# A residual block in fp32: the second FFN with four plain tiles instead of five, x's block sums by accumulating DMAs, transposes in runs of eight

## The chip, the cores and the metric

The kernel runs on one core of one Trainium2 chip. The metric is the device time of one execution in microseconds; the time given for a kernel is the median of its runs.

## The reference

One layer of a streaming encoder, S = 512 tokens, D = 1024, FF = 2816, all in fp32:

```
x = x + 1/2 * swiglu_ffn(rmsnorm(x, ffn1_norm), ffn1_w_gate, ffn1_w_up, ffn1_w_down)
x = x + hybrid_mixer(rmsnorm(x, mix_norm), ...)      # attention in chunks and pooling, one output projection
x = x + 1/2 * swiglu_ffn(rmsnorm(x, ffn2_norm), ffn2_w_gate, ffn2_w_up, ffn2_w_down)
x = rmsnorm(x, final_norm)

rmsnorm(x, g)    = x * rsqrt(mean(x * x) + 1e-6) * g
swiglu_ffn(x)    = (silu(x @ w_gate) * (x @ w_up)) @ w_down
```

## The kernel before

Every product is taken in three matmuls (`mm3`, L208 to L210): each operand is split into a rounded part `hi` (ScalarE casts it, L154 or L157) and a rest `lo` (VectorE subtracts, L155 or L158), and hi x hi, lo x hi and hi x lo are accumulated.

Each FFN's up half works through 22 column tiles f of 128 gate and 128 up columns. The tiles come in two kinds. A **plain** tile takes eight k-steps of gate and eight of up, each on 512 tokens: 48 matmuls of 512 columns. A **half-size** tile treats gate and up as the columns of a 2 x 2 block product and uses seven block products instead of eight (A11, S1, S2, S3, A12, A22, S4, in Winograd's form): 84 matmuls of 256 columns. For that it needs sums of x's blocks, S1 = a21 - a22, S2 = S1 + a11, S3 = a11 + a21 and S4 = S2 - a12 up to signs, and of the weights' blocks. `PLAIN = (5, 5)` says how many tiles of either FFN are plain; the others are half-size.

The change is in the second FFN's **opening**: all its plain tiles, the norm's sums, and whatever the first half-size tile needs. Its order on TensorE, VectorE and ScalarE is the string `OPENING`, written out by hand, a token a step. `W i` splits weights i, `B i` is a block of the first two tiles (two k-steps of both, 24 matmuls), `P` one half (gate or up) of a later plain tile, `L` a quarter of the last one; `n` is a step of the norm, whose last writes `rb`, the factor of each token; `g`, `u`, `m` are a tile's gate, its up, and the sums of its output; `h` prepares the first half-size tile's weights, `F` fetches some, `O` opens output tiles. `p` takes one step off the list that `Norm.blocks` returns: eight scalings of x by rb and the gain into the tiles `aside` (L403), the sums of blocks, and the splits of S3 and S2 (tiles `xa`), S4 (`sa`) and of A11, A22, S1, A12 (`ha`, two instructions each for hi and lo).

After the opening the half-size tiles follow in a loop with its own written order. In each, `u` is copied from the bank of the first product (ScalarE, L721) before the third product adds to that bank.

While the opening runs, TensorE also transposes the x that came from the mixer: 32 transposes `by_token` (L1666), taken one by one off the list `further` by `block` and `last_block`, four into a bank, which ScalarE copies (L1671) and SP stores to `x_d`. GpSimd's queue carries the sums of the down weights in DRAM: `make_sums` issues a mark and two DMAs (L868) a tile, some of them accumulating, as `RATES` says.

Of the kernel before, what the change touches and what calls it, by code (L numbers as in the profile page):

```python
# [12 lines left out]
AF = mybir.ActivationFunctionType  # L13
ALU = mybir.AluOpType
# [6 lines left out]
KD = D // P  # L21
# [17 lines left out]

ROOM, AHEAD_OF_PARTS, ALIGN = 1024 + 128, 16, 64  # L40
OFF, OFF_AT = (0, 2, 6), 32
PLAIN = (5, 5)
RATES = [[2] * (n - 1) + [0] + [2] * (FF // P - n - 2) + [0] * 2 for n in PLAIN]
PROBS = 3
M_TILES = 16
# [14 lines left out]
ACT_FIX, DVE_FIX, QK_NORM, NORM = 0.09, 0.1, 3.7538, 3.08  # L60
AHEAD_AT = 8
OPENING = (
    "W1 n0 B0 n1 W2 n2 B1 W3 p B2 p p p p p p W4 p B3 g0 p g1 p u0 W5 u1 p m0 m1 O1 W6 W7 p p P20 P21 W8 "
    "P30 g2 p u2 m2 p P31 W9 g3 u3 m3 F0 F1 L0 h0 F2 h1 F3 L1 p h2 L2 p h3 p L3 h4 g4 h5 F4 p O0 "
)
AHEAD, NORM_AT, FILL_AT, QK_ROOT = 2, 3, 7, ()
RANKS = {
# [8 lines left out]
def layer(  # L76
# [225 lines left out]
    class Norm:  # L302
# [80 lines left out]
            nc.vector.scalar_tensor_tensor(self.rb, v, 1.5, y, op0=ALU.add, op1=ALU.mult)  # L383
            yield

        def blocks(self, pool, aside):

            x_lo, x_hi = (z[:, : 4 * S].rearrange("p (k c) -> p k c", c=S) for z in aside[:2])
            a11, a21 = x_lo[:, :, :HT], x_lo[:, :, HT:]
            a12, a22 = x_hi[:, :, :HT], x_hi[:, :, HT:]
            s2, s4, s1 = (
                z[:, at : at + 4 * HT].rearrange("p (k c) -> p k c", c=HT)
                for z, at in ((aside[0], 4 * S), (aside[1], 4 * S), (aside[2], 0))
            )
            self.a = [None] * 7  # L400

            def scale(k):
                nc.vector.scalar_tensor_tensor(  # L403
                    (x_lo, x_hi)[k // 4][:, k % 4], x[k], gain_sb[:, self.which, k : k + 1],
                    self.rb, op0=ALU.mult, op1=ALU.mult,
                )

            def add(dst, one, two, op):
                nc.vector.tensor_tensor(dst, one, two, op=op)

            def whole(i, src, make, sign=None):
                pair = [make().rearrange("p (k c) -> p k c", c=HT) for _ in range(2)]
                split(src, *pair, sign)
                self.a[i] = [[z[:, k] for k in range(4)] for z in pair]

            def halves(i, src):

                self.a[i] = [[], []]
                for k in (0, 2):
                    pair = [  # L420
                        hpool.tile([P, 2, HT], F32R, tag="h", name=name("ha")) for _ in range(2)
                    ]
                    split(src[:, k : k + 2], *pair)
                    for z, to in zip(pair, self.a[i]):
                        to.extend(z[:, j] for j in range(2))

            def by_x(i):
                return lambda: xpool.tile([P, 2 * S], F32R, tag=f"x{i.pop()}", name=name("xa"))

            def extra():  # L430
                return pool.tile([P, 4 * HT], F32R, tag="extra", name=name("sa"), bufs=2)

            free = [3, 2, 1, 0]
            return [(scale, k) for k in range(KD)] + [
                (add, s1, a21, a22, ALU.subtract),
                (add, s2, s1, a11, ALU.add),
                (add, a21, a11, a21, ALU.add),
                (whole, S3, a21, by_x(free), -1.0),
                (whole, S2, s2, by_x(free), -1.0),
                (add, s4, s2, a12, ALU.subtract),  # L440
                (whole, S4, s4, extra),
                (halves, A11, a11),
                (halves, A22, a22),
                (halves, S1, s1),
                (halves, A12, a12),
            ]


    def ffn_up(norm, wA, down, loaded, parts=(), aside=(), further=()):
# [24 lines left out]
        def block(w, kp):  # L474
            for kk in range(2):
                k = 2 * kp + kk
                for j in range(4):
                    mm3(first[j], cut(w, (kk * 4 + j) * P, P), norm.h[k], k == 0, k == KD - 1)
                    if kp:
                        for _ in range(min(1 + (j == 3), len(further))):  # L480
                            further.pop(0)()

        def nothing():
            pass
# [1 line left out]
        def blocks_of(aside=()):  # L486
            aside = list(aside) + [
                down.pool.tile(
                    [P, 6 * groups[g][1] * HT], F32, tag=f"acts{groups[g][0]}", name=name("aside")
                )  # L490
                for g in range(G - 3 + len(aside), G)
            ]
            todo.extend(norm.blocks(down.pool, aside))

        def read_in():
            for kp in range(KD // 2):
# [79 lines left out]
        def opening():  # L576

            banks, halves_of = {f: first[2 * f : 2 * f + 2] for f in range(2)}, {}
            raw = dict(enumerate(parts[1:], 1))
            w = {0: parts[0]}  # L580
            steps = norm.steps()

            def fetch_raw(i):
                if i < 2 * plain and i not in raw:
                    raw[i] = raw_of(wA[i])

            def prepare(i):
                w[i] = parts_of(raw[i])
                fetch_raw(i + 3)

            def last_block():
                for j in range(4):
                    for kk in range(2):
                        k = KD - 2 + kk
                        mm3(first[j], cut(w[3], (kk * 4 + j) * P, P), norm.h[k], False, k == KD - 1)
                        for _ in range(min(1 + kk, len(further))):
                            further.pop(0)()

            def tile_product(n, j):
                acc = bank()  # L600
                banks.setdefault(n, []).append(acc)
                for k in range(KD):
                    mm3(acc, cut(w[2 * n + j], k * P, P), norm.h[k], k == 0, k == KD - 1)

            def last_tile(part):
                n = plain - 1
                if part == 0:
                    banks[n] = [bank(), bank()]
                for k in range(2 * part, 2 * part + 2):
                    for j in range(2):  # L610
                        mm3(
                            banks[n][j], cut(w[2 * n + j], k * P, P), norm.h[k], k == 0, k == KD - 1
                        )

            def gate(f):
                g, sg = temp(), temp()
                nc.vector.tensor_tensor(g, banks[f][0], norm.rb, op=ALU.mult)
                nc.scalar.activation(sg, g, AF.Silu)
                halves_of[f] = sg

            def up(f):
                sg = halves_of[f]
                nc.vector.tensor_tensor(sg, sg, norm.rb, op=ALU.mult)
                down.place(f, banks[f][1], sg)

            def sums(f):
                down.sums(f)
                down.make_sums(halves_of[f], 2)

            def half_size(what):  # L630
                n = plain
                if what == 0:
                    high11(n)
                    low11(n)
                elif what == 1:
                    sum13(n)
                elif what == 2:
                    high13(n)
                    low13(n)
                elif what == 3:  # L640
                    sum24(n)
                elif what == 4:
                    high24(n)
                else:
                    low24(n)

            def loads(what):
                fetch(plain + what // 2, ("ra", "rb")[what % 2])

            do = {  # L650
                "W": prepare, "B": lambda i: block(w[i], i) if i < 3 else last_block(),
                "P": lambda i: tile_product(i // 10, i % 10), "L": last_tile, "g": gate, "u": up,
                "m": sums, "h": half_size, "F": loads, "n": lambda i: next(steps), "p": piece,
                "O": lambda i: down.open(range(1, G - 3) if i else range(G - 3, G)),
            }
            for token in OPENING.split():
                do[token[0]](int(token[1:] or 1))
            assert not todo and not further
            return partial(up, plain - 1), partial(sums, plain - 1)
# [149 lines left out]
    class Down:  # L809
# [37 lines left out]
        def begin(self, pool):  # L847
            self.pool, self.acts = pool, []
            self.raws, self.parts, self.pairs = {}, {}, {}
            self.n_products, self.loads, self.loads_from = 0, [], 4  # L850
            self.open(range(1))
            rooms[:] = [
                z for tag in ("ra", "rb") for z in ((wpool, "raw", RAW, 1024), (pool, tag, RAW, 2 * S))
            ]
            part_rooms[:] = [(wpool, HILO)] * HILO + [(pool, 1)]
# [1045 lines left out]
```

## Time and profile before

| | |
|---|---|
| time, median of 3 runs | 837.81 us (837.65 to 838.47) |
| the profiled execution's own time | 838.23 us |
| its span, first to last instruction | 836.5 us |
| TensorE busy, share of the span | 99% |
| VectorE, ScalarE, GpSimd | 85%, 60%, 18% |
| opening of the second FFN | 501.94 to 560.51 us of the span |
| its 17 half-size tiles | 560.51 to 722.77 us |
| its down half and the end | 722.77 to 836.4 us |

Durations of single instructions are in the timeline's rows; an engine starts the next of its instructions a little before the last one's recorded end, so a row of several gives the distance between two. A DMA's time runs from its issue to its landing.

### The profile page before, as it was taken

What the parts mean: (1) busy time and instruction counts of PE and PEld (TensorE: products, weight loads), DVE (VectorE), ACT (ScalarE), POOL (GpSimd) and SP (SyncE); (2) the same over time, 40 slices, a digit from 0 to 9 for tenths busy, and PEclk for the clock granted to TensorE, in tenths of its full rate; (3) what the DMA queues carried; (4) which work ended last, traced back from release to release, by engine and by line L of the source; (5) the groups of instructions that cost most, each with busy time, mean ns of one, the idle gap of its engine ahead of it and who ended that gap; (6) DMA issues with size and microseconds to landing.
All of it is one profiled execution on the core that took longest, in us unless ns stands there. A gap on an engine that the chain in (4) does not pass through costs nothing.

```text
span 836.5 us, 14350 instructions
## 1 busy us (share of the span) xinstructions
PE 826.8 (99%) x5288; PEld 740.3 (89%) x5288; DVE 712.0 (85%) x1157; ACT 501.8 (60%) x859; POOL 150.0 (18%) x212
## 2 busy tenths in 40 slices
PE   9999999999999999999999999999999999999996
PEld 7889999999988888887888887889999999988885
DVE  7999998899897678766979668989889999887896
ACT  8446555665675656558747745455566555756573
POOL 0312211222074000102111000111221121132600
PEclk9999999999999999999999999999999999999999
DMA  8667788888689973332221137757877888689922
GB/s 300 183 198 170 200 210 243 201 207 207 193 245 271 329 233 110 108 110 89 76 69 62 67 110 263 235 154 216 215 212 217 214 204 211 228 269 340 323 87 101
DMA packets 78839, 160.63 MB, mean 192 GB/s; under 512 B 7328, under 2 KB 30384, under 8 KB 78384
## 3 DMA queue, kind: packets, MB, share of 16 engines
q1 hardware_dynamic: 55680, 113.03, 40.1%
q0 software_dynamic: 22656, 46.14, 26.0%
q8 instruction: 41, 0.67, 0.3%
q10 hardware_dynamic: 432, 0.54, 0.2%
q14 instruction: 30, 0.25, 0.1%
HBM read 153.38 MB, written 50.34 MB: 244 GB/s over the span
## 4 chain that ended last, share of the span: by engine, by line
PE 97%; DMA 1%; DVE 1%; ACT 0%; SPq 0%; issue 0%; DVEq 0%
PE mm L208 23%; PE mm L210 23%; PE mm L209 23%; PE a L208 8%; PE a L209 8%; PE a L210 8%; PE a L1438 1%; PE a L1374 1%; PE a L1426 1%; DMA x<-in_xT_dram 1%; PE a L1296 0%; PE a L1666 0%; PE a L327 0%; PE a L1029 0%; PE mm L1029 0%; SPq L201 0%
## 5 line engine op out<-in xcount | busy, mean ns | idle before, releaser
L155 DVE TENSOR_TENSOR wlo<-raw,whi 128x1024 fp32r<-128x1024 f32 (+2 forms) x115 | 124.4, 1088 | 25.9 <-ACT whi L154 25.3
L154 ACT CAST whi<-raw 128x1024 fp32r<-128x1024 f32 (+2 forms) x115 | 107.3, 944 | 49.2 <-PE mm L210 13.0
L209 PE MATMUL mm<-ha,whi 128*128 128x256 f32 x408 | 112.8, 276 | 0.0
L208 PE MATMUL mm<-ha,whi 128*128 128x256 f32 x408 | 112.8, 276 | 0.0
L210 PE MATMUL mm<-ha,wlo 128*128 128x256 f32 x408 | 112.7, 276 | 0.0
L721 ACT ACTIVATE t<-mm 128x256 f32<-128x256 f32 x102 | 39.2, 384 | 114.3 <-PE mm L210 111.6
L531 DVE TENSOR_TENSOR wlo<-wsum,whi 128x1024 fp32r<-128x1024 f32 x68 | 83.0, 1220 | 11.0 <-PE mm L210 7.9
L866 POOL COPY mark<-t 128x1 f32<-128x1 f32 x44 | 14.3, 324 | 391.6 <-DVE t L774 243.0
L208 PE MATMUL mm<-hhi,whi 128*128 128x512 f32 x192 | 76.6, 401 | 0.9 <-ACT whi L154 0.6
L209 PEld LDWEIGHTS mm<-ha,whi 128*128 128x128 f32 x408 | 76.6, 188 | 0.1
L208 PEld LDWEIGHTS mm<-ha,whi 128*128 128x128 f32 x408 | 76.6, 188 | 0.1
L210 PEld LDWEIGHTS mm<-ha,wlo 128*128 128x128 f32 x408 | 76.6, 188 | 0.0
L209 PE MATMUL mm<-hlo,whi 128*128 128x512 f32 x192 | 74.9, 391 | 0.0
L210 PE MATMUL mm<-hhi,wlo 128*128 128x512 f32 x192 | 74.8, 391 | 0.0
L868 POOL DMA_DIRECT2D wsum<-in_wB_dram x72 | 71.1, 1102 | 12.3 <-issue 7.5
L526 ACT CAST whi<-wsum 128x1024 fp32r<-128x1024 f32 x68 | 67.9, 1047 | 2.0 <-PE mm L209 1.5
L209 PE MATMUL mm<-wlo,ah 128*128 128x512 f32 x176 | 68.5, 389 | 0.0
L210 PE MATMUL mm<-whi,ah 128*128 128x512 f32 x176 | 68.5, 389 | 0.0
L208 PE MATMUL mm<-whi,ah 128*128 128x512 f32 x176 | 68.4, 389 | 0.0
L531 DVE TENSOR_TENSOR wlo<-raw,whi 128x512 fp32r<-128x512 f32 x68 | 62.0, 950 | 0.0
L526 ACT CAST whi<-raw 128x512 fp32r<-128x512 f32 x68 | 56.2, 827 | 2.5 <-issue 2.5
L208 PE MATMUL a<-whi,ah 128*128 128x512 f32 (+1 forms) x154 | 55.7, 362 | 0.0
(233 smaller groups left out, 2398.7 us busy)
## 6 DMA issues: line engine op xcount, KB each, us to landing
raw<-in_wA_dram SPq DMA_DIRECT2D x136, 256.0 KB, 4.1
wsum<-in_wB_dram POOLq DMA_DIRECT2D x60, 512.0 KB, 6.9
raw<-wsum SPq DMA_DIRECT2D x40, 512.0 KB, 4.8
raw<-in_wB_dram SPq DMA_DIRECT2D x30, 512.0 KB, 7.4
wsum<-wsum POOLq DMA_DIRECT2D x20, 512.0 KB, 5.2
raw<-in_wA_dram SPq DMA_DIRECT2D x19, 512.0 KB, 4.1
x<-in_xT_dram SPq DMA_DIRECT2D x16, 256.0 KB, 8.8
raw<-in_wQK_dram SPq DMA_DIRECT2D x8, 512.0 KB, 3.5
```

The costliest lines, as they stand in the source:

```text
L154: nc.scalar.copy(hi, src)
L155: nc.vector.tensor_tensor(lo, src, hi.bitcast(F32), op=ALU.subtract)
L208: nc.tensor.matmul(acc, a[0], b[0], start=start, stop=False, **more)
L209: nc.tensor.matmul(acc, a[0], b[1], start=False, stop=False, **more)
L210: nc.tensor.matmul(acc, a[1], b[0], start=False, stop=stop, **more)
L526: nc.scalar.copy(hi, src)
L531: nc.vector.tensor_tensor(lo, src, hi.bitcast(F32), op=ALU.subtract)
L721: nc.scalar.activation(dst, src, AF.Copy, scale=scale)
L866: nc.gpsimd.tensor_copy(mark, after[:, 0:1])
L868: nc.gpsimd.dma_start(self.rows(i, g), self.rows(self.terms[i][at], g), **(dict(accum_op=ALU.add) if at else {}),)
L1374: nc.tensor.matmul(banks[i][:, at : at + n], qT[pair][0][a][rows, t * P : (t + 1) * P], kT[pair][0][b][rows, :n], start=a + b == 0, stop=a ...
L1426: nc.tensor.transpose(tp[:, n : n + P], prob[h, t][:, j * P : (j + 1) * P], ident)
```

## The change

The second FFN has four plain tiles and eighteen half-size ones; the first FFN is as it was. `blocks` gets a second list for the second FFN: each sum of blocks is begun by a scaled copy on ScalarE (`begin`) and completed by one accumulating DMA from SBUF to SBUF on GpSimd's queue (`onto`); S3 is added into a21 in place. `OPENING` is written anew for one tile fewer, and `block` takes eight transposes after each k-step of blocks 1 and 2, none in the last.

```diff
-PLAIN = (5, 5)
+PLAIN = (5, 4)
@@
-    "W1 n0 B0 n1 W2 n2 B1 W3 p B2 p p p p p p W4 p B3 g0 p g1 p u0 W5 u1 p m0 m1 O1 W6 W7 p p P20 P21 W8 "
...
+    "W1 n0 W2 B0 n1 W3 n2 p2 B1 B2 p8 W4 p2 B3 g0 p g1 u0 m0 u1 p W5 O1 W6 W7 p2 P20 P21 p g2 m1 F0 "
...
@@ blocks
+            def begin(dst, src, sign):
+                nc.scalar.activation(dst, src, AF.Copy, scale=sign)
+
+            def onto(dst, src):
+                nc.gpsimd.dma_start(dst, src, accum_op=ALU.add)
+
             free = [3, 2, 1, 0]
+            if by_dma:
+                return [(scale, k) for k in range(KD)] + [
+                    (begin, s1, a22, -1.0),
+                    (onto, s1, a21),
+                    (begin, s2, a11, 1.0),
+                    (onto, a21, a11),
+                    (onto, s2, s1),
+                    (begin, s4, a12, -1.0),
+                    (whole, S3, a21, by_x(free), -1.0),
+                    (whole, S2, s2, by_x(free), -1.0),
+                    (onto, s4, s2),
+                    (whole, S4, s4, extra),
+                    (halves, A11, a11),
+                    (halves, A22, a22),
+                    (halves, S1, s1),
+                    (halves, A12, a12),
+                ]
@@ block
-                    if kp:
-                        for _ in range(min(1 + (j == 3), len(further))):
-                            further.pop(0)()
+                for _ in range(min(2 * NT if kp else 0, len(further))):
+                    further.pop(0)()
@@ blocks_of
-            todo.extend(norm.blocks(down.pool, aside))
+            todo.extend(norm.blocks(down.pool, aside, loaded))
@@ last_block
-                        for _ in range(min(1 + kk, len(further))):
-                            further.pop(0)()
```

What moves, at three places. First TensorE, in block 1 of the opening, before (`xr` is the x to be transposed, `mm` the banks of the first two tiles, `a` the bank of transposes):

```order
L354 MATMUL a_6082<-t_6081,ones_r 128x512
L208 MATMUL mm_6066<-hhi_5953,whi_6074 128x512
L209 MATMUL mm_6066<-hlo_5954,whi_6074 128x512
L210 MATMUL mm_6066<-hhi_5953,wlo_6075 128x512
L1666 MATMUL a_6131<-ident_r,xr_6049 128x128
L208 MATMUL mm_6067<-hhi_5953,whi_6074 128x512
L209 MATMUL mm_6067<-hlo_5954,whi_6074 128x512
L210 MATMUL mm_6067<-hhi_5953,wlo_6075 128x512
L1666 MATMUL a_6131<-ident_r,xr_6049 128x128
```

And now, at the end of block 1's first k-step:

```order
L208 MATMUL mm_6069<-hhi_5953,whi_6074 128x512
L209 MATMUL mm_6069<-hlo_5954,whi_6074 128x512
L210 MATMUL mm_6069<-hhi_5953,wlo_6075 128x512
L1686 MATMUL a_6148<-ident_r,xr_6049 128x128 x4
L1686 MATMUL a_6156<-ident_r,xr_6049 128x128 x4
L208 MATMUL mm_6066<-hhi_5963,whi_6074 128x512
L209 MATMUL mm_6066<-hlo_5964,whi_6074 128x512
```

The transposes, one or two after every third matmul before, now stand eight together after twelve matmuls, and fill two banks at once.

Second GpSimd's queue in the opening, before (`mark` waits for a tile's gate or up; `wsum` are the down weights' sums in DRAM):

```order
L866 COPY mark_6307<-t_6285 128x1
L868 DMA wsum_138<-in_wB_dram 256x1x512
L868 DMA wsum_139<-in_wB_dram 256x1x512
L866 COPY mark_6316<-t_6290 128x1
L868 DMA wsum_138<-in_wB_dram 256x1x512
L868 DMA wsum_140<-in_wB_dram 256x1x512
```

And now (`aside_6051` holds a11, a21 and s2, `aside_6070` a12, a22 and s4, `aside_6071` s1):

```order
L437 DMA aside_6071<-aside_6051 128x4x256
L437 DMA aside_6051<-aside_6051 128x4x256
L437 DMA aside_6051<-aside_6071 128x1024
L886 COPY mark_6301<-t_6289 128x1
L888 DMA wsum_138<-in_wB_dram 256x1x512
L888 DMA wsum_139<-in_wB_dram 256x1x512
L437 DMA aside_6070<-aside_6051 128x1024
L886 COPY mark_6390<-t_6294 128x1
L888 DMA wsum_138<-in_wB_dram 256x1x512
```

Three adds stand ahead of the first mark, the fourth (S4's) behind the first two copies of the down weights' sums; what followed the marks before now follows the adds.

Third ScalarE at the end of the opening, before (`whi` from `wsum` or `raw` are the first half-size tile's weights, `t` from `t` a gate's silu, `t` from `mm` u's copy):

```order
L154 CAST sa_6434<-aside_6070 128x1024
L154 CAST whi_6463<-raw_6327 128x1024
L618 ACTIVATE t_6468<-t_6467 128x512
L526 CAST whi_6502<-raw_6482 128x512
L154 CAST ha_6527<-aside_6051 128x512
L154 CAST ha_6531<-aside_6051 128x512
L526 CAST whi_6535<-wsum_6509 128x1024
```

And now:

```order
L154 CAST sa_6431<-aside_6070 128x1024
L154 CAST ha_6441<-aside_6051 128x512
L154 CAST ha_6445<-aside_6051 128x512
L548 CAST whi_6473<-wsum_6428 128x1024
L154 CAST ha_6480<-aside_6070 128x512
L154 CAST ha_6484<-aside_6070 128x512
L154 CAST ha_6488<-aside_6071 128x512
L154 CAST ha_6492<-aside_6071 128x512
L548 CAST whi_6496<-wsum_6477 128x1024
L638 ACTIVATE t_6512<-t_6511 128x512
L154 CAST ha_6516<-aside_6070 128x512
L154 CAST ha_6520<-aside_6070 128x512
```

The split of S4, which stood ahead of the last plain tile's weights, now stands ahead of the splits of the other four operands and of the weight sums, and it reads what the fourth add writes; u's copy, in the row after the last shown, stands behind them all.

More of the change, by code (lines that the diff above doesn't have):

```diff
@@ L62 @@
 OPENING = (
-    "W1 n0 B0 n1 W2 n2 B1 W3 p B2 p p p p p p W4 p B3 g0 p g1 p u0 W5 u1 p m0 m1 O1 W6 W7 p p P20 P21 W8 "
-    "P30 g2 p u2 m2 p P31 W9 g3 u3 m3 F0 F1 L0 h0 F2 h1 F3 L1 p h2 L2 p h3 p L3 h4 g4 h5 F4 p O0 "
+    "W1 n0 W2 B0 n1 W3 n2 p2 B1 B2 p8 W4 p2 B3 g0 p g1 u0 m0 u1 p W5 O1 W6 W7 p2 P20 P21 p g2 m1 F0 "
+    "u2 m2 L0 F1 h0 h1 p F2 F3 p L1 L2 h2 h3 p2 h4 L3 g3 h5 p F4 O0 "
 )
@@ L384, in steps, with blocks @@
             yield
-        def blocks(self, pool, aside):
+        def blocks(self, pool, aside, by_dma=False):
             x_lo, x_hi = (z[:, : 4 * S].rearrange("p (k c) -> p k c", c=S) for z in aside[:2])
```

## The prediction

> **What bounds the kernel now.** The page comes first: how busy each engine is, and the chain of work that ended last.
>
> ```profile
> PE 826.8 (99%) x5288; PEld 740.3 (89%) x5288; DVE 712.0 (85%) x1157; ACT 501.8 (60%) x859; POOL 150.0 (18%) x212
> PE 97%; DMA 1%; DVE 1%; ACT 0%; SPq 0%; issue 0%; DVEq 0%
> ```
>
> TensorE is never idle for long and the chain is TensorE's: time goes only where it gets fewer or shorter matmuls, and comes only where another engine makes it wait. So I cut the span where the change lies, in the table of busy time by stretch (columns: length, then busy time and count of PE, PEld, DVE, ACT, POOL, then clock, DMA share and GB/s).
>
> ```profile
> 501.94:560.51 58.57, 58.57 (x275) 47.62 (x274) 51.42 (x65) 29.62 (x41) 6.77 (x12) 1.00 0.74 232
> 560.51:722.77 162.26, 162.26 (x1429) 162.26 (x1428) 148.07 (x225) 96.02 (x174) 29.13 (x48) 1.00 0.77 205
> 541.02:551.90 10.88, 10.88 (x50) 9.01 (x48) 8.39 (x12) 4.41 (x6) 2.65 (x5) 1.00 0.73 203
> ```
>
> The first row is the opening of the second FFN (five plain tiles, the norm's sums, 32 transposes), the second its 17 half-size tiles. PE is busy for all of both. The third row is one plain tile's length: 48 matmuls of 512 columns between two starts (the two further ones counted reach in from the ends), 10.88 us, 0.2267 each. A half-size tile takes 162.26 / 17 = 9.545 us for 84 matmuls, 0.1136 each. In the opening VectorE is busy for 51.42 of 58.57 us: it is the engine that would run out if the opening were simply made shorter.
>
> **The change part by part.** *One plain tile goes, one half-size tile comes*: -10.88 + 9.545 = **-1.3 us** of TensorE.
>
> *Transposes in runs of eight.* Where they stand now, in the timeline of PE (start, time, line, count); the last two rows are runs of four elsewhere in the program, on plain fp32:
>
> ```profile
> 507.38 0.62 PE L354 MATMUL a<-t,ones_r 128*128 128x512 f32 x2
> 507.84 0.39 PE L208 MATMUL mm<-hhi,whi 128*128 128x512 f32 x1
> ...
> 508.59 0.44 PE L208 MATMUL mm<-hhi,whi 128*128 128x512 f32 x1
> ...
> 509.40 0.45 PE L208 MATMUL mm<-hhi,whi 128*128 128x512 f32 x1
> ...
> 510.21 0.45 PE L208 MATMUL mm<-hhi,whi 128*128 128x512 f32 x1
> ...
> 510.96 0.28 PE L1666 MATMUL a<-ident_r,xr 128*128 128x128 f32 x2
> 511.08 0.46 PE L208 MATMUL mm<-hhi,whi 128*128 128x512 f32 x1
> ...
> 368.18 0.60 PE L1296 MATMUL a<-ident,t 128*128 128x128 f32 x4
> ...
> 369.32 0.60 PE L1296 MATMUL a<-ident,t 128*128 128x128 f32 x4
> ```
>
> From 508.59 to 509.40 lie three matmuls (0.68) and one transpose: 0.81, so a lone transpose costs 0.13. From 510.21 to 511.08 lie three matmuls and two transposes: 0.87, so the second costs 0.06. The norm's two sums take 507.84 - 507.38 = 0.46. All 32 transposes now cost 58.57 - 240 x 0.2267 - 0.46 = 3.7. A run of eight would cost 0.13 + 7 x 0.06 = 0.55, four runs 2.2. The other bound: the fp32 runs of four take 369.32 - 368.18 - 0.68 = 0.46, 0.115 each, and 32 of those are the 3.7 of now. I take the row of the same kind of transpose: **-1.5 us**, and keep 0 for the range.
>
> Without any wait the opening then ends 192 x 0.2267 + 0.46 + 2.2 = 46.2 us after 501.94, at 548.1, and the sum is -1.3 - 1.5 = **-2.8 us**.
>
> *The four adds leave VectorE.* They take 1.21 us each there; with two fewer weight splits (1.22 each) and one gate and up fewer VectorE loses some 9 of its 51.4 us while the opening shrinks by 12.4. That is what makes four plain tiles possible. ScalarE gains three copies (1.05 each) and loses two casts. The price is that three of the four adds now follow each other through the DMA queue: s1, then s2 = s1 + a11 (queued behind the add into a21), then s4 = s2 + a12. No run shows an accumulating DMA from SBUF to SBUF; the nearest rows of the DMA list are (out<-in, KB each, us from issue to landing):
>
> ```profile
> wsum<-in_wB_dram POOLq DMA_DIRECT2D x1, 512.0 KB, 4.3
> wsum<-in_wB_dram POOLq DMA_DIRECT2D x1, 512.0 KB, 6.4
> wsum<-in_wB_dram POOLq DMA_DIRECT2D x1, 512.0 KB, 7.8
> xr<-x SPq DMA_DIRECT2D x8, 256.0 KB, 2.6
> raw<-in_wA_dram SPq DMA_DIRECT2D x2, 256.0 KB, 3.5
> wsum<-in_wB_dram POOLq DMA_DIRECT2D x1, 512.0 KB, 6.6
> wsum<-in_wB_dram POOLq DMA_DIRECT2D x2, 512.0 KB, 7.5
> ```
>
> ```profile
> 616.56 2.13 POOL L868 DMA_DIRECT2D wsum<-in_wB_dram  x2 [0.25 <-issue]
> ```
>
> The rows are answers for short stretches of time. The first (529.8 to 530.3 us) is a plain copy on GpSimd's queue, the second (569.4 to 570.0) an accumulating one with little beside it, the third (534.3 to 534.9) an accumulating one beside SP's weight fetches. The fourth and fifth say what SBUF instead of DRAM saves: 2.6 against 3.5. The last two are a pair of accumulating ones, the first alone (6.6) and both (median 7.5, so the second took 8.4); GpSimd's timeline has them issued within 2.13 us, about 0.9 apart, so the second lands some 2.7 behind the first. So an add costs between 4.3 (adding is free) and 7.8; I take 6.4 less some 0.8 for SBUF, and 0.2 more for the fetches beside it: **5.8 us**, nearest to the 6.4.
>
> Now the walk. The first two blocks after the norm's sums end at 501.94 + 72 x 0.2267 + 0.46 + 2.2 = 520.9, and ScalarE copies the last transposes before it starts s1. These are the rows of ScalarE and VectorE on which this and the rest lie (where xN stands, N instructions run into each other; in brackets idle time ahead of a row and what ended it):
>
> ```profile
> 528.00 0.59 ACT L1671 COPY t<-a 128x512 f32<-128x512 f32 x1 [1.16 <-PE a L1666]
> 529.53 2.94 ACT L154 CAST whi<-raw 128x1024 fp32r<-128x1024 f32 x3
> 542.59 1.06 ACT L154 CAST sa<-aside 128x1024 fp32r<-128x1024 f32 x1 [0.45 <-DVE aside L409]
> 546.86 0.63 ACT L618 ACTIVATE t<-t 128x512 f32<-128x512 f32 x1 [2.26 <-DVE t L617]
> 561.33 1.13 ACT L154 CAST ha<-aside 128x512 fp32r<-128x512 f32 x2
> 562.36 0.37 ACT L721 ACTIVATE t<-mm 128x256 f32<-128x256 f32 x1
> 515.21 0.69 DVE L383 SCALAR_TENSOR_TENSOR rb<-t,t 128x512 f32<-128x512 f32 x1
> 516.95 4.73 DVE L403 SCALAR_TENSOR_TENSOR aside<-x,gain_sb,rb 128x512 f32<-128x512 f32 x7
> 535.07 2.35 DVE L155 TENSOR_TENSOR wlo<-raw,whi 128x1024 fp32r<-128x1024 f32 x2
> 541.35 1.21 DVE L409 TENSOR_TENSOR aside<-aside,aside 128x1024 f32<-128x1024 f32 x1
> 553.16 1.28 DVE L155 TENSOR_TENSOR ha<-aside,ha 128x512 fp32r<-128x512 f32 x2
> 560.03 0.69 DVE L617 TENSOR_TENSOR t<-mm,rb 128x512 f32<-128x512 f32 x1 [0.65 <-PE mm L210]
> ```
>
> The copy ends near 521.7, s1's start (1.05) at 522.8; VectorE's eight scalings (4.73 for seven, so 0.66 apart) follow rb, there at 515.9, and end at 521.2, in time. The first add lands at 522.8 + 5.8 = 528.6, the second at 534.4, the third 2.7 behind it at 537.1. The fourth is queued on GpSimd behind a mark and two 512 KB copies of the down weights' sums; these drain while it starts, and it lands at 537.1 + 5.8 = **542.9**.
>
> Behind it waits ScalarE, in a written order: S4's split (1.06), then eight casts of halves, two casts of weight sums, the last gate's silu and the copy of u. On VectorE stand S4's rest (2.35 - 1.22 = 1.13), two halves (0.6 each), a weight sum's rest 1.13, two sums (1.2), four halves (2.4), the last gate (0.69); then ScalarE's silu 0.54 until the next can start, two casts (1.03) and u's copy (0.37). In sum 1.06 + 1.13 + 1.2 + 1.13 + 1.2 + 2.4 + 0.69 + 0.54 + 1.03 + 0.37 = 10.8, with hops of about 0.1 between engines 11.1. TensorE's third product writes on into the bank that u's copy reads, so it cannot start before 542.9 + 11.1 = 554.0. By itself it would start two products after the opening: 548.1 + 24 x 0.1136 = 550.9. So TensorE waits **3.1 us** there. VectorE, 91% busy in this stage (148.07 of 162.26), then catches up over the next tile; 0.3 us for that.
>
> The other three adds are covered: what waits for a21 and s2 (S3's and S2's splits on ScalarE, at 528.6 to 537) has 11 us of plain tile left on TensorE. GpSimd's marks and eight DMAs for the down weights are queued behind the adds by some 10 us; their readers start at 722.77, so nothing ends on them. SP's stores of the turned x now come in pairs; they are read after 722.77 too.
>
> Sum: -1.3 - 1.5 + 3.1 + 0.3 = **+0.6 us**. The profiled execution took 838.23 us (span 836.5), 0.42 above the median of 837.81. So 838.8 for a profiled one, and **838.4 us** as median. About 0.2% (1.7 us) is what a measurement of this kernel can tell from no change.
>
> **The rivals.** *Adds at the forecast's price or near it* (5.2 to 6.2): each 0.1 us of an add counts three times in the walk, so 836.6 to 839.6. For it: the rows of the same operation. Chance 0.48.
>
> *Adds as quick as copies*: at 4.7 us or less the fourth lands by 539.7, the third product is ready at 550.8, and no wait is left: 837.81 - 2.8 = **835.0**. For it: the plain copy's 4.3 and SBUF's lesser latency; the schedule's order of steps leaves about that much room. Against it: every accumulating row is above 6. Chance 0.20. The Trainium skill, DMA: Bandwidth & Descriptors, section on the anatomy of one DMA on the gpsimd path, prices a DMA at 2.0 us plus its bytes over 436 GB/s, an estimate of 3.2 us for 512 KB; by that rule this rival would hold. The trace's plain copy, at 4.3, lies above it.
>
> *Adds late, TensorE waits longer than the removed tile saves*: at 6.6 us each the fourth lands at 522.8 + 3 x 6.6 + 2.7 = 545.3, the third product starts at 556.4, the wait is 5.5, the sum +3.0: **840.8**; at 7.8 it is 844.4. The point from which it decides is an add of 6.2. For it: the 7.8 beside fetches, and half-size weights are fetched in just these microseconds (DMA share 0.74). Against: SBUF at both ends. Chance 0.25.
>
> *The runs of eight cost what 32 single ones cost*, with weight loads one after the other (the 0.115 of the fp32 runs): opening +1.5, part of which covers the wait; about 839.9. Chance 0.07.
>
> **How the numbers follow.** Faster by over 0.2% is the quick adds, 0.20. Slower by over 0.2% are the late adds, the dear runs, and the upper end of the forecast's case (0.06): 0.38. The rest, 0.42, is within 0.2%. The range goes from 834.9 (no wait at all) to 842.2 (adds of about 7), leaving out some 0.05 below and 0.1 above.
>
> **What would show it.** In the profile after: half-size matmuls first at 46 us after the opening's start; the four adds in the list of DMAs with some 5.8 us to landing; PE's first idle time over 0.2 us in the first half-size tile, before its third product, released by ScalarE's copy of u; the transposes as four rows of x8. The forecast is wrong if PE has no idle time there (quick adds), if it is 5 us or more (late adds), or if PE waits in the opening itself, which nothing here foresees.

## The result, and the profile after

| | before | after |
|---|---|---|
| time, median | 837.94 us (837.65 to 838.47, 4 runs) | 844.78 us (844.18 to 845.01, 4 runs) |
| the profiled execution: span | 836.5 us | 843.0 us |
| from the opening's start to the down half's start | 220.83 us | 227.81 us |

The changed kernel is slower: ratio 1.0075, 95% interval 1.0063 to 1.0086. The forecast was 838.4 with a range up to 842.2, so it missed by 6.4 us, on the side of the rival "adds late".

In the rows below PE is TensorE, PEld its weight loads, DVE VectorE, ACT ScalarE and POOL GpSimd. The page, first and fourth part: TensorE is still busy for 98%, but the chain of work that ended last now runs through DMAs for 3% of the span.

```profile
PE 829.1 (98%) x5324; PEld 745.2 (88%) x5324; DVE 711.4 (84%) x1160; ACT 506.7 (60%) x869; POOL 154.6 (18%) x216
PE 94%; DMA 3%; DVE 1%; issue 0%; ACT 0%; POOL 0%; DVEq 0%; ACTq 0%; POOLq 0%
```

The table of busy time by stretch, cut at the opening's start, the last plain matmul, the start of the third product, the end of the slow matmuls behind it, and the down half's start (columns: length, PE busy and count, granted clock, DMA share, GB/s):

```profile
501.67:548.68 47.01, 47.01 (x227) 1.00 0.86 239
548.68:558.82 10.14, 4.78 (x26) 0.83 0.84 225
558.82:562.46 3.64, 3.64 (x17) 0.53 0.14 25
562.46:729.48 167.02, 167.02 (x1474) 1.00 0.80 212
```

The opening has no wait; it takes 47.01 us. The 24 matmuls of the first two products would take 24 x 0.1136 = 2.73 us and are given 10.14: the third product is 7.41 us late. The next 17 matmuls take 3.64 us instead of 1.93, at a granted clock of 0.53. Then TensorE is full to the end. The timeline of PE in the second and third of these stretches:

```profile
548.45 0.39 PE L210 MATMUL mm<-hhi,wlo 128*128 128x512 f32 x1
549.42 0.38 PE L208 MATMUL mm<-ha,whi 128*128 128x256 f32 x1 [0.59 <-ACT ha L154]
550.77 0.38 PE L209 MATMUL mm<-ha,whi 128*128 128x256 f32 x1 [0.96 <-DVE ha L155]
552.21 0.42 PE L208 MATMUL a<-xa,whi 128*128 128x256 f32 x1
552.42 0.42 PE L209 MATMUL a<-xa,whi 128*128 128x256 f32 x1
554.60 0.41 PE L210 MATMUL a<-xa,wlo 128*128 128x256 f32 x1
558.82 0.58 PE L208 MATMUL mm<-xa,whi 128*128 128x256 f32 x1 [3.80 <-ACT t L741]
```

The largest wait is the one that the forecast named, before the third product, released by the copy of u. Two smaller ones stand in the first product: 549.42 - 548.68 = 0.74, and 1.24 behind its first matmul. From 552.0 to 554.6, ahead of the third product, and from 558.8 to 562.2, in it and behind it, matmuls of 256 columns start 0.21 apart instead of 0.114. Now the adds. The list of DMA issues, in answers for short stretches: the first add, the second, the second and third together (the median of two), the fourth.

```profile
aside<-aside POOLq DMA_DIRECT2D x1, 512.0 KB, 6.3
aside<-aside POOLq DMA_DIRECT2D x1, 512.0 KB, 6.7
aside<-aside POOLq DMA_DIRECT2D x2, 512.0 KB, 8.3
aside<-aside POOLq DMA_DIRECT2D x1, 512.0 KB, 5.8
```

Issue to landing: 523.83 to 530.11, 530.65 to 537.34, 531.42 to 541.42, 542.00 to 547.78. Where the forecast had 5.8 for each, 2.7 between the second and the third, and 542.9 for the last landing, there are 6.3 and 6.7, 4.1 between the second and the third, about 0.55 each time between a landing and the next issue, and 547.8. What VectorE and ScalarE did meanwhile, from their timelines:

```profile
529.53 3.49 DVE L155 TENSOR_TENSOR wlo<-raw,whi 128x1024 fp32r<-128x1024 f32 x3
538.46 1.22 DVE L158 SCALAR_TENSOR_TENSOR xa<-aside,xa 128x1024 fp32r<-128x1024 f32 x1 [5.44 <-ACT xa L157]
542.54 1.23 DVE L158 SCALAR_TENSOR_TENSOR xa<-aside,xa 128x1024 fp32r<-128x1024 f32 x1 [2.86 <-ACT xa L157]
543.68 0.68 DVE L637 TENSOR_TENSOR t<-mm,rb 128x512 f32<-128x512 f32 x1
548.89 1.22 DVE L155 TENSOR_TENSOR sa<-aside,sa 128x1024 fp32r<-128x1024 f32 x1 [0.48 <-ACT sa L154]
556.11 0.69 DVE L637 TENSOR_TENSOR t<-mm,rb 128x512 f32<-128x512 f32 x1
541.45 1.06 ACT L157 ACTIVATE xa<-aside 128x1024 fp32r<-128x1024 f32 x1 [3.02 <-DMA aside<-aside]
547.80 1.05 ACT L154 CAST sa<-aside 128x1024 fp32r<-128x1024 f32 x1 [2.21 <-DMA aside<-aside]
558.39 0.37 ACT L741 ACTIVATE t<-mm 128x256 f32<-128x256 f32 x1
```

Read with the forecast's eyes, the chain looks as it said: the fourth add lands at 547.78, ScalarE splits S4 at 547.80, and 11.0 us behind the landing the copy of u is done. But VectorE tells something else too. It stands idle for 5.44 us ahead of S3's split and 2.86 ahead of S2's, and behind those two splits in its queue is the gate of the third plain tile (543.68), whose product TensorE had finished some 11 us earlier (in the experiment on order, below, the same gate ran at 532.80). From 548.89 on it has no idle time until the last gate at 556.11, which the copy of u waits for through ScalarE. So there are two readings. **Theory A**: the fourth add's landing sets the third product. **Theory B**: VectorE's queue sets it, held up by the second and third adds; S4 could come earlier and nothing would change. A third, **theory C**: VectorE has too much work for four plain tiles, whatever the order.

### The profile page after: what moved, and what is told of

Its sections match the earlier page's. It is cut to its first block, busy times and chain, and to the rows that moved or that the text cites. A ratio compares the mean times of both kernels' runs of the same rounds, so it can differ in the third digit from the quotient of the medians.

```text
span 843.0 us, 14423 instructions
## 1 busy us (share of the span) xinstructions
PE 829.1 (98%) x5324; PEld 745.2 (88%) x5324; DVE 711.4 (84%) x1160; ACT 506.7 (60%) x869; POOL 154.6 (18%) x216
## 4 chain that ended last, share of the span: by engine, by line
PE 94%; DMA 3%; DVE 1%; issue 0%; ACT 0%; POOL 0%; DVEq 0%; ACTq 0%; POOLq 0%
PE mm L208 22%; PE mm L210 22%; PE mm L209 22%; PE a L209 8%; PE a L208 8%; PE a L210 8%; DMA aside<-aside 3%; PE a L1458 1%; PE a L1394 1%; PE a L1446 1%; PE a L247 0%; PE a L1316 0%; DVE ha L155 0%; PE a L1686 0%; DMA x_d<-t 0%
## 5 line engine op out<-in xcount | busy, mean ns | idle before, releaser
L155 DVE TENSOR_TENSOR wlo<-raw,whi 128x1024 fp32r<-128x1024 f32 (+2 forms) x113 | 122.2, 1089 | 29.1 <-ACT whi L154 28.6
L154 ACT CAST whi<-raw 128x1024 fp32r<-128x1024 f32 (+2 forms) x113 | 105.1, 941 | 50.8 <-PE mm L210 14.6
L209 PE MATMUL mm<-ha,whi 128*128 128x256 f32 x420 | 116.4, 277 | 1.0 <-DVE ha L155 1.0
L208 PE MATMUL mm<-ha,whi 128*128 128x256 f32 x420 | 116.3, 277 | 0.6 <-ACT ha L154 0.6
L210 PE MATMUL mm<-ha,wlo 128*128 128x256 f32 x420 | 116.3, 277 | 0.0
L553 DVE TENSOR_TENSOR wlo<-wsum,whi 128x1024 fp32r<-128x1024 f32 x70 | 85.5, 1221 | 11.7 <-ACT whi L548 7.1
L209 PEld LDWEIGHTS mm<-ha,whi 128*128 128x128 f32 x420 | 78.9, 188 | 1.2 <-DVE ha L155 1.2
L208 PEld LDWEIGHTS mm<-ha,whi 128*128 128x128 f32 x420 | 78.9, 188 | 1.1 <-ACT ha L154 1.0
L210 PEld LDWEIGHTS mm<-ha,wlo 128*128 128x128 f32 x420 | 78.9, 188 | 0.0
L208 PE MATMUL mm<-hhi,whi 128*128 128x512 f32 x176 | 69.6, 399 | 0.0
L209 PE MATMUL mm<-hlo,whi 128*128 128x512 f32 x176 | 68.6, 391 | 0.0
L210 PE MATMUL mm<-hhi,wlo 128*128 128x512 f32 x176 | 68.6, 391 | 0.0
```

What stands on the lines that cost most here:

```text
L154: nc.scalar.copy(hi, src)
L155: nc.vector.tensor_tensor(lo, src, hi.bitcast(F32), op=ALU.subtract)
L208: nc.tensor.matmul(acc, a[0], b[0], start=start, stop=False, **more)
L209: nc.tensor.matmul(acc, a[0], b[1], start=False, stop=False, **more)
L210: nc.tensor.matmul(acc, a[1], b[0], start=False, stop=stop, **more)
L553: nc.vector.tensor_tensor(lo, src, hi.bitcast(F32), op=ALU.subtract)
```

## Experiments

**The last add on VectorE.** From the changed kernel:

```diff
-                    (begin, s4, a12, -1.0),
...
+                    (add, s4, s2, a12, ALU.subtract),
                     (whole, S2, s2, by_x(free), -1.0),
-                    (onto, s4, s2),
```

> The changed kernel, but the last of the four adds (s4 = s2 - a12) is done by VectorE as soon as s2 has landed, ahead of the split of S2; the copy that begins s4 and its DMA go. Theory A, the fourth add's landing (547.5 where 542.9 was forecast) is what makes the third product late: S4 is ready at about 542.5 instead of 547.5, the third product comes some 4.6 us earlier, and the time falls from 844.8 to about 840 or below (838.5 if the low clock behind the wait goes too). Theory B, VectorE's queue is what is late (it stood idle 5.4 and 2.9 us at the head of the splits of S3 and S2, with gates and weight splits queued behind, and from then to the third product it is busy without a break): S4's early landing gains nothing, since VectorE still has the same work to do after the third add lands at 541.2; the fourth add's DMA turns into 1.2 us of VectorE. Third product within 1 us of 558.8, time 843 to 845.

844.75 us, ratio to the kernel before 1.0074 (1.0058 to 1.0090): nothing gained. Timeline of VectorE, ScalarE and PE:

```profile
539.79 1.23 DVE L158 SCALAR_TENSOR_TENSOR xa<-aside,xa 128x1024 fp32r<-128x1024 f32 x1 [6.28 <-ACT xa L157]
542.58 1.22 DVE L409 TENSOR_TENSOR aside<-aside,aside 128x1024 f32<-128x1024 f32 x1 [1.56 <-DMA aside<-aside]
545.62 0.63 ACT L637 ACTIVATE t<-t 128x512 f32<-128x512 f32 x1 [1.98 <-DVE t L636]
546.67 1.05 ACT L154 CAST sa<-aside 128x1024 fp32r<-128x1024 f32 x1
558.90 0.58 PE L208 MATMUL mm<-xa,whi 128*128 128x256 f32 x1 [3.02 <-ACT t L740]
```

S4 is summed by 543.8 instead of 547.8. ScalarE splits it only at 546.67, behind the third tile's silu, which waits for VectorE's gate, which waited for the adds. The third product starts 56.72 us after the opening's start (502.18) instead of 57.15. The second and third adds landed later here, by 0.8 and 0.6 us counted from the opening's start, which can hide no more than that of the 4.6 that theory A promised. Theory A falls.

**Two adds on VectorE.** Only s1 and a21 go by DMA, and S2 and S4 no longer wait for any add behind them. `OPENING` was fitted to the new list, with both sums and the splits of S2, S3 and S4 ahead of the third tile's gate, so the written order differs too:

```diff
-                    (begin, s2, a11, 1.0),
                     (onto, a21, a11),
-                    (onto, s2, s1),
-                    (begin, s4, a12, -1.0),
+                    (add, s2, s1, a11, ALU.add),
+                    (whole, S2, s2, by_x(free), -1.0),
+                    (add, s4, s2, a12, ALU.subtract),
                     (whole, S3, a21, by_x(free), -1.0),
-                    (whole, S2, s2, by_x(free), -1.0),
-                    (onto, s4, s2),
```

> The changed kernel, but only two adds go by DMA (s1 and a21); s2 = s1 + a11 and s4 = s2 - a12 are done by VectorE once s1 has landed, and S2 and S4 are prepared before and beside S3. Nothing waits for more than two adds in a row: S3's split can start at about 537.4 as now, S2's at 531. Theory A (the fourth add's landing decides): S4 is there before 538, no wait is left, about 835 to 836. Theory B (VectorE's queue): it is held only until the second add lands (537.1) instead of until the third (541.2), so its work is done some 4 us earlier and the third product starts about 4.5 us earlier, with a wait of some 2 to 3 us left: 839 to 840.5, less if the low clock behind the wait goes too.

839.95 us, ratio 1.0024 (1.0015 to 1.0032): as theory B had it. VectorE's waits from 520 to 549 (what waited, on what; sum, times, longest):

```profile
DVE wlo L156 <- ACT whi L155: 3.2, 1, 3.2
DVE xa L159 <- ACT xa L158: 2.5, 2, 1.3
```

The waits at the two splits are 2.5 us where they were 8.3, although VectorE has two more adds to do. TensorE's wait before the third product is 2.5.

**The same instructions in another order.** As the first experiment, with three adds by DMA, and this part of the written order:

```diff
-... W5 O1 W6 W7 p2 P20 P21 p g2 m1 F0 u2 m2 L0 F1 h0 h1 p F2 F3 p
+... W5 O1 W6 W7 P20 P21 g2 m1 F0 F1 h0 p u2 m2 p p p h1 L0 F2 F3 p
```

> As e1_last_add (three adds by DMA, the last one by VectorE), with the same instructions, and the written order changed: the third plain tile's gate and its sums, and the first half-size tile's weights, stand ahead of the splits of S3 and S2 on VectorE and ScalarE instead of behind them. The DMAs land as before (second add near 537.5, third near 541.5), so S4 is ready no earlier than in e1. Theory B (VectorE held at the head of its queue by waits for adds, 8.3 us, with work behind it that was ready): the idle time is filled, the third product starts some 4 us earlier than in e1, and the time is 840 to 841. Theory C (VectorE simply has too much work for four plain tiles, the order does not matter) or theory A (the adds' landing): as e1, 844 to 845.

840.53 us, ratio 1.0022 (1.0013 to 1.0031): 4 us less than the first experiment by order alone. Its VectorE's waits, then its PE:

```profile
DVE xa L159 <- ACT xa L158: 2.9, 1, 2.9
DVE aside L410 <- DMA aside<-aside: 0.6, 1, 0.6
DVE wlo L553 <- ACT whi L548: 0.5, 1, 0.5
554.56 0.56 PE L209 MATMUL mm<-xa,whi 128*128 128x256 f32 x1 [3.03 <-ACT t L741]
```

The second and third adds landed at 537.25 and 541.52, as late as ever (537.34, 541.42). The third product starts 53.0 us after the opening's start (501.56) instead of 56.7. So the adds' landing cost most of what it did because ready work stood behind it: theory B.

**No copies beside the adds.** In the changed kernel, the down weights' DMAs of the first two tiles put off:

```diff
+RATES[1][:12] = [0, 0] + [2, 0] + [2] * 4 + [3] * 4
```

> The changed kernel with the down weights' DMAs of the first two tiles put off to later tiles (as many in all), so that no DMA of 512 KB from DRAM stands on GpSimd's queue beside the second, third and fourth add. If the copies made the third add late (4.1 us behind the second, forecast 2.7): it lands 1.4 us earlier, and so do VectorE's queue and the third product: 843.4. If the adds themselves take that long, one behind the other on the queue: third add 4.1 behind the second again, 844.5 to 844.8.

844.27 us, ratio 1.0071 (1.0058 to 1.0083). The second add, the second and third, and the fourth:

```profile
aside<-aside POOLq DMA_DIRECT2D x1, 512.0 KB, 6.5
aside<-aside POOLq DMA_DIRECT2D x2, 512.0 KB, 8.0
aside<-aside POOLq DMA_DIRECT2D x1, 512.0 KB, 5.7
```

The third lands 3.8 us behind the second, not 2.7: an add of 512 KB within SBUF takes the queue some 4 us, copies or none. The weight fetches on SP's queue went on beside them.

**The runs of eight alone**, in the kernel before:

```diff
-                    if kp:
-                        for _ in range(min(1 + (j == 3), len(further))):
-                            further.pop(0)()
+                for _ in range(min(2 * NT if kp else 0, len(further))):
+                    further.pop(0)()
@@ last_block
-                        for _ in range(min(1 + kk, len(further))):
-                            further.pop(0)()
```

> The kernel before with one thing changed: the transposes in runs of eight behind each k-step of blocks 1 and 2, none in the last block. The forecast's step: 32 transposes cost 2.2 instead of 3.7 us, so 1.5 us faster than before, 836.4. From the trace of the changed kernel: its opening is 47.0 us for 192 matmuls of 0.2267 and 0.46 of sums, which leaves 3.0 for the transposes, so 0.7 faster: 837.2. The rival that runs of eight cost what single ones cost: no change, 837.9.

837.48 us beside 838.17 for the kernel before, ratio 0.9991 (0.9983 to 1.0000). Opening and half-size tiles:

```profile
501.77:559.63 57.86, 57.86 (x275) 1.00 0.75 235
559.63:721.90 162.27, 162.27 (x1430) 1.00 0.79 205
```

57.86 - 240 x 0.2267 - 0.46 = 3.0 us for 32 transposes, 0.75 for a run, where 0.55 was forecast: 0.7 us gained, not 1.5.

**Filler for the wait.** The changed kernel with throwaway matmuls on the otherwise idle TensorE:

```diff
+                if n == plain and loaded:
+                    fill(up_lo, 18)
                 product(acc, w11, A11, True)
...
+                if n == plain and loaded:
+                    fill(up_lo, 40)
                 product(acc, cut(w24, 0, S), S2, False)
```

> The changed kernel, with 58 matmuls of 256 columns added whose results are thrown away: 18 ahead of the first half-size tile's first product and 40 ahead of its third, 6.6 us in sum at 0.1136 each. They stand where TensorE waits now (6.0 us, and 1.4 of slow matmuls between the waits), so no product should start later. If the wait lowers the clock, and the slow matmuls behind it (560 to 562.4, some 0.21 apart instead of 0.114) are its consequence, the clock stays at 1.0, and 1.7 us are saved: about 843.1. If the low clock there has another cause, nothing is saved: 844.8, or up to 1 us more where the filler runs over.

843.72 us, ratio 1.0068 (1.0056 to 1.0080). The stretches that answer to those of the changed kernel:

```profile
549.28:559.38 10.10, 9.99 (x84) 1.00 0.80 220
559.38:562.46 3.08, 3.08 (x26) 1.00 0.11 20
562.46:729.00 166.54, 166.54 (x1465) 1.00 0.81 212
```

The third product is as late as ever (57.10 us after the opening's start), but the clock stays at 1.00 and no matmul is slow. From the opening to the down half it takes 226.72 us instead of 227.81, 1.1 us less, where 1.7 were expected. The last stretch lost some 0.5 that the changed kernel does not lose there; by what was not followed up. So the low clock cost at least 1.1 us by the traces; the times alone (ratio 1.0068 beside 1.0075) do not tell the two kernels apart. Not every wait brought a low clock. It was 0.51 behind the wait of 3.0 in the order experiment, and 1.00 behind the wait of 2.5 with two adds on VectorE:

```profile
554.56:558.00 3.44, 3.44 (x16) 0.51 0.77 137
```

```profile
554.38:558.00 3.62, 3.53 (x28) 1.00 0.20 36
```

The changed kernel's own clock, with the span cut where the granted clock changes:

```profile
548.61:552.02 3.41, 1.86 (x13) 1.00 1.05 294
552.02:555.43 3.41, 2.99 (x15) 0.50 0.78 262
555.43:558.85 3.42, 0.04 (x1) 1.00 0.70 120
558.85:562.26 3.41, 3.41 (x16) 0.50 0.14 26
```

There are two low stretches of 3.41 us each, one behind the two small gaps and one behind the long wait, with the clock back at 1.00 between them while TensorE stood idle. The first lies ahead of the third product, where TensorE had to wait anyhow; only the second cost time.

The Trainium skill, TensorE: Matmul & The Clock Gate, section on what's actually happening, has the clock halved after an idle window of about 3.4 us that runs freely. The halving agrees. In the changed kernel, though, matmuls were slow from 552.0 on, after gaps of 0.74 and 1.24 us with one matmul between them, which no whole idle window fits into; nor does one fit into the wait of 3.0 in the order experiment.

**The sums by GpSimd's own adds**, and that with a better order:

```diff
-                    (begin, s1, a22, -1.0),
-                    (onto, s1, a21),
...
+                    (pool_add, s1, a21, a22, ALU.subtract),
+                    (pool_add, s2, s1, a11, ALU.add),
+                    (pool_add, a21, a11, a21, ALU.add),
+                    (pool_add, s4, s2, a12, ALU.subtract),
...
+            def pool_add(dst, one, two, op):
+                nc.gpsimd.tensor_tensor(dst, one, two, op=op)
```

> The changed kernel with the four sums made by GpSimd's own tensor_tensor instead of a copy on ScalarE and an accumulating DMA each. GpSimd's adds of 527 columns take 1.07 us elsewhere in this program, so 1024 columns are estimated at 2.1 us, against 6 to 10 us from issue to landing for a DMA. S4 is there before 535 and VectorE waits for none. Theory B: no wait is left in the first half-size tile, and the time is the forecast's sum without its wait, with the transposes' measured gain: -1.3 - 0.7 = -2.0 against before, about 836.0. Theory C (VectorE's amount of work): a wait of 3 us or more stays, 839 or more. If VectorE is slowed while GpSimd adds, up to 1 us more than theory B.

838.06 us beside 838.39, ratio 0.9996 (0.9987 to 1.0004): 6.7 us less than the changed kernel, and 2 short of theory B's number. GpSimd's fourth add; VectorE in answers for short stretches, so that each instruction stands by itself; and PE:

```profile
530.02 2.87 POOL L434 TENSOR_TENSOR aside<-aside,aside 128x1024 f32<-128x1024 f32 x1
528.44 2.19 DVE L637 TENSOR_TENSOR t<-t,rb 128x512 f32<-128x512 f32 x1
530.73 0.69 DVE L892 TENSOR_TENSOR acts<-mm,t 128x512 f32<-128x512 f32 x1
531.34 2.64 DVE L155 TENSOR_TENSOR wlo<-raw,whi 128x1024 fp32r<-128x1024 f32 x1
534.03 0.50 PE L210 MATMUL mm<-hhi,wlo 128*128 128x512 f32 x1 [0.83 <-DVE wlo L155]
```

A weight split that VectorE starts while GpSimd adds takes 2.64 us instead of 1.22: it goes on for its usual time after GpSimd's add has ended (532.89). The product of 0.69 in the middle, which reads a bank of TensorE's, is not held. The Trainium skill, SBUF — State Buffer, section on the two separate sides, says that an instruction of VectorE with two SBUF inputs and one of GpSimd exclude each other for their whole length; these rows agree.

The order was then changed to keep the weights' splits ahead of the held instructions:

```diff
-... u0 m0 u1 p W5 O1 W6 W7 p2 P20 P21 ... h0 h1 p F2 F3 p L1 L2 h2 h3 p2 h4 L3 g3 h5 p
+... u0 m0 p W5 O1 W6 W7 u1 p2 P20 P21 ... h0 F2 F3 h1 p2 L1 p L2 h2 h3 p h4 L3 g3 h5 p
```

> As e6_pool_adds, with the written order changed in a few places: the splits of the fourth plain half's and of the last tile's weights stand ahead of the second tile's up on VectorE (in e6 TensorE waited 0.8 us for such a split, slowed by GpSimd's adds), and S1's halves behind the split of the sums' weights. If that wait was all that kept four plain tiles from paying: 0.8 us off e6, some 1.2 us below the kernel before, 837.2 where that takes 838.4. If VectorE, slowed while GpSimd adds, is late at another place instead: no change from e6 (0.9996 of the kernel before).

838.32 us beside 838.46, ratio 1.0001 (0.9992 to 1.0010). PE's only wait, and VectorE from 530 to 550:

```profile
PE mm L209 <- ACT t L736: 1.2, 1, 1.2
530.00:540.00 10.00, 9.93 (x11) 1.00 0.62 192
540.00:550.00 10.00, 9.86 (x16) 1.00 0.85 231
```

The wait in the opening is gone, and 1.2 us came back before the third product. The opening takes 46.98 us and the eighteen half-size tiles 173.94, where 18 x 9.545 would be 171.81: the 2.1 us lost there eat up what the removed tile and the runs of eight save (1.3 and 0.7). Of them 1.2 are the wait; the rest is in no wait on the list. VectorE is now full for 20 us, so this may be the limit that theory C speaks of; no run with less work for VectorE puts it to the test. No version with four plain tiles beat five. The fastest kernel of the study is the one before with the runs of eight, by 0.7 us, at the edge of what was measured.

## Why the prediction was wrong

The forecast's sum was +0.6 us, the stage's change is 227.81 - 220.83 = +7.0.

- *One tile for another, -1.3*: nothing contradicts it. The opening of 47.01 us and the full stretches at clock 1.00 are as this term has them.
- *Transposes, -1.5*: mis-sized. The opening of 47.01 us leaves them 3.0, not 2.2: -0.7. Taking the second of a pair (0.06) as the price of all seven that follow was too low.
- *TensorE's wait, +3.1*: right place, right releaser, wrong size and wrong cause. It is 7.41. Two steps failed. The first is the walk's prices: an add at 5.8 and 2.7 behind another, where 5.7 to 7.5 and 3.5 to 4.3 were measured over these runs, and nothing for the 0.55 between a landing and the next issue. So the last landing came 4.9 us late, and 554.0 + 4.9 + 11.0 - 11.1 gives the third product at 558.8, which fits the trace and is still not the cause. The step that failed outright is "The other three adds are covered". It looked at what TensorE had left, not at what stood behind the waiting splits on VectorE. The last-add experiment shows that summing S4 4 us earlier brings the third product forward by only 0.4; the order experiment shows that filling VectorE's idle time gains 4 us with the adds as late as before.
- *Catching up, +0.3*: it is 7.0 + 1.3 + 0.7 - 7.4 = 1.6, and the low clock behind the wait, which the forecast did not have, accounts for all of it: the 17 slow matmuls took 3.64 us instead of 1.93. The filler gave 1.1 back.
- *The rivals.* "Adds late" came nearest. Its formula, at the 7.3 us an add that the last landing implies ((547.8 - 523.26 - 2.7) / 3, from the measured end of s1's beginning), gives 842.9; the transposes' 0.8, which puts s1 off, and the low clock make up the rest. Its mechanism, by the fourth add, is the one that fell. "Runs of eight dear" is out: they are 0.7 cheaper. "Quick adds", put to the test with GpSimd's adds, removed the waits on the adds, but VectorE was held instead and TensorE waited 0.8 for a weight split in the opening: 838.1, not 835.0. The rule of the Trainium skill, DMA: Bandwidth & Descriptors, section on the anatomy of one DMA, by which that rival would have held (an estimate of 3.2 us), does not fit here: every add took 5.7 us or more.

## What to carry to other kernels

When an operation moves to a slower but otherwise idle unit, walk every in-order queue that holds a waiting reader, and list what is ready behind it: the price is the idle time of that engine, if it has none to spare, and not the lateness of the last result. VectorE was 88% busy in the opening before (51.42 of 58.57 us), so it had little to spare. From the last-add experiment to the one on order its waits behind 530 us fell from 7.9 us (6.3 and 1.6) to 4.0 (2.9, 0.6 and 0.5), and TensorE's third product came 3.7 us earlier. A chain that fits the measured end is not shown by fitting: here two chains ended within 0.5 us of each other, and only taking one away told them apart.

## What the hardware showed

- An accumulating DMA of 512 KB within SBUF took 5.7 to 7.5 us from issue to landing where none was ahead of it, and a second one issued 0.8 us later landed 3.5 to 4.3 behind the first. That is about what accumulating ones from DRAM took in the kernel before (6.4 and 6.6).
- A GpSimd add of 128x1024 took 2.87 us; VectorE's instructions with two SBUF inputs waited for its end.
- Two gaps of 0.74 and 1.24 us with one matmul between them were enough to bring TensorE's clock to half for 3.41 us; a single wait of 2.5 in another run was not. Why is open.
- A run of eight transposes between matmuls took 0.75 us, 32 spread ones 3.7 in all.
